# A bidirectional hybrid encoder layer: the start of the kernel in another order, with the conditioning row by transfer, one shift column on TensorE, h in pairs, and x of groups 2 and 3 issued later

## Chip, cores and metric

One core of a Trainium2 chip runs the kernel. The metric is the device time of one execution, in microseconds. A run of a kernel's time is the median of several executions; the profile is of one more execution, and its span goes from the first to the last instruction.

## The reference, cut to what matters

One layer over 2048 tokens of 1024 channels. The part that the change touches is the modulated norm at the layer's start and the first columns of the input projection:

```python
c_act = silu(c)
mod = c_act @ w_ada + b_ada
shift, scale, gate = split(mod, 3)
h = rmsnorm(x, norm_w) * (1.0 + scale) + shift
proj = h @ w_in + b_in                  # 4624 columns
# neighbourhood attention and a chunked two-way mLSTM on parts of proj
y = concatenate([na_out, ml_out]) @ w_out
out = rmsnorm(x + gate * y, final_norm_w)
```

`norm_w` times 1 + scale is called `gT` below, one number for each channel, and shift `shT`. Both are needed before h, and h before any product of the projection.

## The kernel before

The tokens go in four groups of 512 (four tiles of 128 each), the channels in eight pieces of 128, called k. A matrix product in float32 is made of three products of rounded parts: h is held as `hhi` and `hlo`, a weight block as `whi` and `wlo`, and a result is the sum of hi·hi, hi·lo and lo·hi. The input projection goes through weight blocks of 256 columns. Blocks 0, 1 and 2 (values and output gates of the mLSTM heads) are first; block 0 carries the 16 gate columns beside it and is 272 wide.

`start` makes the h of all four groups and applies these first blocks. It is written under a manual schedule: each engine does its instructions in the order of the Python lines. After it, a scheduler orders the instructions by dependence.

The conditioning. The scale and shift of piece k are dot products of silu(c) with 128 columns of `w_ada`. They arrive as 16 pieces of 512 KB (`load_mod(n)`, n = 2k for the scale and 2k + 1 for the shift), in 11 places of which five are used twice. `mod(n)` is one VectorE instruction with a reduction (`dot`, L264) over a piece whose rows are channels and whose 1024 columns meet the silu(c) row, which therefore has to lie in all partitions: `c_all`. In the kernel before, the row comes into one partition (`crow`, L324), gets its Silu, goes to all partitions by two TensorE products with a row of ones (L356), and two ScalarE copies take it out of PSUM (L366). For k = 0 both numbers come from TensorE instead: 8 matmuls of one column each (L381), each in two passes, on matrix pieces laid out the other way. Around these stand filler matmuls (`warm`, L350): 14, then 3, then 2, which write a tile that nothing reads.

Group 0. x is scaled by the norm's factor, turned by TensorE (`turned(k)`, L392, two pieces ahead), and ScalarE makes `hhi` and h from the turned x with gT and shT (`first_h`, L399); VectorE makes `hlo` (L400). `products(k)` (L426) does 24 matmuls for piece k, on blocks 0 (`a`) and 1 (`b`): first those with hhi, then those with hlo. VectorE also does the dots for the next piece and the low parts of the weights (L320).

Groups 1 to 3. x comes a second time, transposed (`load_t`, L254), beside the rows for the norm (`load_x`, L248). `spread` puts the norm's factors in all partitions by four matmuls with a diagonal (L290). `make_h` is three steps for each piece: VectorE multiplies (L406), ScalarE adds the shift and rounds (`hhi`, L407), VectorE takes the difference (`hlo`, L408). They are called from `next_h` for pieces 0 to 3, between the tiles of the block before, and singly for 4 to 7. Tiles for h have two buffers.

Evictions and stores. `vo_group` adds the bias on VectorE (L672) into a staging tile (two exist, used in turn), ScalarE applies a Sigmoid (L678), and the tile is stored to `d_ck`: for group 0 at once, from ScalarE's queue (L681), else later from SP's (L683). An eviction into a staging tile waits until the store before has left it. For group 0 three blocks follow each other (0, 1, 2); for the others two, and block 2 comes again later for groups 1 to 3.

SP issues most transfers, in the order of the program; `table_fills` (L714) are large writes of a constant to DRAM that lie between them. A transfer waits for an earlier one that uses the same of eight semaphores, so up to eight are under way.

## Time and profile before

| | us |
|---|---|
| median of 3 runs | 1343.73 |
| lowest, highest | 1339.22, 1345.5 |
| the profiled execution | 1341.4 |
| its span | 1339.3 |
| TensorE busy in the span | 1290.9 |
| VectorE busy in the span | 796.4 |

How to read the lines below. In the windows view each row is a stretch of the span; the engines stand in the order PE (TensorE's matmuls), PEld (its weight loads), DVE (VectorE), ACT (ScalarE), POOL (GpSimd), each with busy time and number of instructions; then the granted TensorE clock as a share, the mean busy share of the 16 DMA engines and their GB/s. In the timeline each row has start, length, engine, source line, operation, what is written and read, the shape, and how many alike were merged; in brackets the engine's idle time before it and what ended that. SPq and ACTq are issues of transfers. A matmul in float32 appears as two records unless it turns a tile. Mean lengths of matmuls overlap: the distance of their starts is what one costs.

### The profile page before, as it was taken

Reading aid. Unit: us, or ns where it says so; the run is one execution under the profiler, and the core shown is the slowest. Engines: PE = TensorE matmul, PEld = TensorE weight load, DVE = VectorE, ACT = ScalarE, POOL = GpSimd, SP = SyncE. Lnnn points to the kernel's source line nnn. Section 1 sums busy time; section 2 is a strip of 40 time slices with the busy share of each in tenths; the row PEclk is TensorE's granted clock in tenths of the full one; section 3 lists DMA queues with packets and bytes.
Section 4 is the critical chain, followed back from the end, with each engine's and each line's share of the span. In section 5 each row is a group of like instructions: output and inputs, shape, how many; then the busy total and the mean of one; then the engine's idle time right before and its main releaser. Section 6 shows DMA issues by size and latency. Waiting matters only on the chain.

```text
span 1339.3 us, 23091 instructions
## 1 busy us (share of the span) xinstructions
PE 1290.9 (96%) x8174; PEld 1103.9 (82%) x8174; DVE 796.4 (59%) x2447; ACT 537.9 (40%) x1176; POOL 194.3 (15%) x255
## 2 busy tenths in 40 slices
PE   8988899999999999999999999999998999999996
PEld 7888899999888787888878888888876777778785
DVE  4855453222545569166767878777547676766663
ACT  4533331644223233123323323333356555565551
POOL 0000100434000000001212002212202211212211
PEclk8989999999999999999999999999999999999998
DMA  9698883999637685545656867656679877868871
GB/s 363 236 285 248 221 233 101 226 221 236 178 92 222 157 204 163 173 119 150 201 157 202 244 192 220 208 163 181 204 249 229 213 193 194 197 176 193 188 185 47
DMA packets 236822, 263.34 MB, mean 197 GB/s; under 512 B 31127, under 2 KB 192279, under 8 KB 236708
## 3 DMA queue, kind: packets, MB, share of 16 engines
q1 hardware_dynamic: 151758, 188.87, 50.0%
q0 software_dynamic: 20496, 36.21, 11.2%
q10 hardware_dynamic: 64454, 36.80, 9.5%
q8 instruction: 64, 1.05, 0.3%
q14 instruction: 50, 0.41, 0.1%
HBM read 177.28 MB, written 92.72 MB: 202 GB/s over the span
## 4 chain that ended last, share of the span: by engine, by line
PE 66%; DMA 12%; DVE 8%; issue 7%; ACT 5%; POOL 1%; SPq 1%; ACTq 0%; DVEq 0%; POOLq 0%
PE pq L1043 18%; PE y L1622 11%; PE pc L601 4%; PE pc L600 4%; PE pc L602 4%; DMA tab<-d_t 3%; PE pT L1562 3%; PE pO L1577 2%; PE pS L1534 2%; DMA dec<-d_mneg 2%; PE pvo L600 2%; PE pvo L601 2%; PE pvo L602 2%; PE px L1282 2%; PE pi L1284 2%
## 5 line engine op out<-in xcount | busy, mean ns | idle before, releaser
L1043 PE MATMUL pq<-hhi,whi_a 128*128 128x512 f32 x512 | 208.2, 407 | 0.8 <-ACT u L948 0.8
L1043 PE MATMUL pq<-hlo,whi_a 128*128 128x512 f32 x512 | 208.4, 407 | 0.0
L1043 PE MATMUL pq<-hhi,wlo_a 128*128 128x512 f32 x512 | 206.7, 404 | 0.0
L1043 PEld LDWEIGHTS pq<-hhi,whi_a 128*128 128x128 f32 x512 | 96.8, 189 | 17.8 <-ACT u L948 1.3
L1043 PEld LDWEIGHTS pq<-hhi,wlo_a 128*128 128x128 f32 x512 | 96.8, 189 | 16.4
L1043 PEld LDWEIGHTS pq<-hlo,whi_a 128*128 128x128 f32 x512 | 96.7, 189 | 16.0 <-issue 0.5
L1564 ACT ACTIVATE pt<-pT 96x384 f32<-96x384 f32 (+3 forms) x128 | 65.9, 515 | 86.1 <-PE pT L1562 83.6
L1543 ACT ACTIVATE pbuf<-pbuf,mn 128x480 f32<-128x480 f32 (+5 forms) x128 | 76.0, 595 | 52.0 <-DVE mn L1542 52.0
L1622 PE MATMUL y<-hhi,whi_a 128*128 128x512 f32 x256 | 91.7, 420 | 0.5 <-ACT whi_a L1592 0.5
L1622 PE MATMUL y<-hhi,wlo_a 128*128 128x512 f32 (+1 forms) x272 | 90.7, 399 | 0.2 <-ACT y L1629 0.2
L1017 POOL TENSOR_TENSOR wlo_a<-rawq,whi_a 128x1024 fp32r<-128x1024 f32 x19 | 45.5, 2396 | 290.8 <-ACT whi_a L1016 277.4
L1542 DVE CUSTOM_DVE_ANT_0 pbuf<-pS,tab 128x480 f32<-128x480 f32 (+5 forms) x128 | 63.0, 540 | 37.2 <-PE pS L1534 31.3
L1287 ACT ACTIVATE num<-px,gtile 128x129 f32<-128x129 f32 x120 | 38.3, 366 | 113.1 <-PE px L1282 83.5
L1562 PEld LDWEIGHTS pT<-ident,pbuf 128*128 128x128 f32 (+2 forms) x416 | 50.9, 137 | 30.0 <-issue 10.5
L1562 PE MATMUL pT<-ident,pbuf 128*128 128x128 f32 (+2 forms) x416 | 67.2, 275 | 8.5 <-DVE pbuf L1554 7.4
L600 PE MATMUL pvo<-whi_b,hhi 128*128 128x256 f32 x224 | 63.7, 285 | 0.0
L1306 POOL TENSOR_TENSOR hm<-hm,ck 128x128 f32<-128x128 f32 x64 | 26.5, 414 | 254.3 <-DVE hm L1305 223.6
L672 DVE TENSOR_TENSOR stvo<-pvo,brow 128x256 f32<-128x256 f32 x60 | 25.0, 422 | 64.4 <-PE pvo L602 54.6
L602 PE MATMUL pvo<-whi_b,hlo 128*128 128x256 f32 x224 | 63.0, 281 | 0.0
L890 ACT ACTIVATE dec<-dec,gtile 128x128 f32<-128x128 f32 x128 | 42.6, 393 | 50.8 <-POOL dec L883 45.8
L601 PE MATMUL pvo<-wlo_b,hhi 128*128 128x256 f32 x224 | 63.0, 281 | 0.0
L635 DVE TENSOR_TENSOR stv<-pv,brow 128x256 f32<-128x256 f32 x32 | 12.8, 422 | 72.7 <-PE pv L602 47.0
(331 smaller groups left out, 3391.5 us busy)
## 6 DMA issues: line engine op xcount, KB each, us to landing
ck<-d_ck SPq DMA_DIRECT2D x64, 384.5 KB
rawq<-in_w_main_dram SPq DMA_DIRECT2D x28, 512.0 KB
raw<-in_w_main_dram SPq DMA_DIRECT2D x18, 512.0 KB
kv<-d_ck SPq DMA_DIRECT2D x64, 128.5 KB
dec<-d_mneg SPq DMA_DIRECT2D x32, 256.0 KB
d_ck<-dec ACTq DMA_DIRECT2D x32, 256.0 KB
d_qna<-qst ACTq DMA_DIRECT2D x32, 256.0 KB
xr<-in_x_dram POOLq DMA_DIRECT2D x15, 512.0 KB, 8.7
```

The costliest lines, as they stand in the source:

```text
L600: nc.tensor.matmul(ps, lhi(k), rhi(k), start=(k == 0), stop=False)
L601: nc.tensor.matmul(ps, lhi(k), rlo(k), start=False, stop=False)
L602: self.mark = nc.tensor.matmul(ps, llo(k), rhi(k), start=False, stop=(k == KT - 1))
L890: nc.scalar.activation(t[:, o, :], t[:, o, :], AF.Exp, bias=self.cols["g"][:, d, h, c : c + 1])
L1017: (eng or nc.gpsimd).tensor_tensor(lo[:, :, cs], raw, hi[:, :, cs].bitcast(F32), ALU.subtract)
L1043: self.mark = nc.tensor.matmul(patch_ps(ps) if patch else ps, w, self.htok(h, g, k, patch), start=(k == 0 and n == 0), stop=(k == KT - 1 a ...
L1287: nc.scalar.activation(num[:, d, :], px[:, d, :], AF.Copy, scale=self.cols["inter"][:, d, h, c : c + 1])
L1542: nc.vector.tensor_tensor_reduce(pt[:, :nk], ps, tabs[place[u]][j][:, :nk], 1.0, 3e38, ALU.add, ALU.min, mn)
L1543: nc.scalar.activation(pt[:, :nk], pt[:, :nk], AF.Exp, bias=mn, scale=-1.0, accum_out=sums[:, j : j + 1])
L1562: nc.tensor.transpose(ps[:cs, i, :], U[u][j][:, i * cs : (i + 1) * cs], self.ident)
L1564: nc.scalar.activation(t[:cs, :nch, :], ps[:cs, :nch, :], AF.Copy)
L1622: nc.tensor.matmul(y, m[:, k, :], w[k][:, cs], start=(k == 4 and n == 0), stop=(k == 3 and n == 2))
```

## The change

1. The conditioning row is no longer spread by TensorE. SP loads it into all 128 partitions at once (a transfer that reads the one row 128 times), behind the first two matrix pieces, the first weight piece and the gate columns. ScalarE applies the Silu to the 128x1024 tile inside the loop, at k = 0. `crow`, its Silu, the two products and the two copies are gone.
2. Of the 19 filler matmuls 5 are left, all at the start.
3. The small VectorE step for `nwb` stands behind the norm's factors instead of ahead of the squares.
4. The shift of piece 1 comes from TensorE: a third column product (piece n = 3, laid out for it on the host) in the middle of `products(0)`, which does all 12 matmuls of block 0 first, then this column, then the 12 of block 1. ScalarE adds the bias. `mod(3)` is gone from VectorE, and `mod(5)` is done at k = 1.
5. `make_h` returns its last step, and `next_h` runs pieces 0 and 1, and 2 and 3, as pairs.
6. `load_x(2)` and `load_t(2)` stand behind the third block of group 0, `load_x(3)` in group 1; the store of that third block goes to SP's queue.

```diff
-        crow = ada.tile([1, D], F32, name="crow")
-        nc.scalar.dma_start(crow, self.c_row)
...
         nc.sync.dma_start(rg, self.w_gate)
+        nc.sync.dma_start(cb, self.c_row.broadcast_to([P, D]))
         load_p(1, 0)
...
-        nc.scalar.activation(crow, crow, AF.Silu)
-        cbs = []
-        for j in range(2):
-            cbs.append(self.tq.tile([P, GT], F32, tag="tp", name=f"cb_{j}"))
-            nc.tensor.matmul(cbs[j], self.ones[0:1, :], crow[:, j * GT : (j + 1) * GT], start=True, stop=True)
-        warm(14)
+        for _ in range(5):
+            nc.tensor.matmul(dense[:, :240], self.ident, self.big, start=True, stop=True)
...
-        nc.vector.scalar_tensor_tensor(nwb, badd[:, KT:], 1.0, nw, ALU.add, ALU.mult)
         for tt in (0, 2):
             square(tt, ssq)
-            if tt == 0:
-                for j in range(2):
-                    nc.scalar.copy(cb[:, j * GT : (j + 1) * GT], cbs[j])
             dot(xt[tt + 1], xt[tt + 1], 1.0, 0.0, ssq[:, tt + 1 : tt + 2])
         rst = roots(four, ssq)
+        nc.vector.scalar_tensor_tensor(nwb, badd[:, KT:], 1.0, nw, ALU.add, ALU.mult)
...
+        def column(to, n):
+            for kt in range(KT):
+                nc.tensor.matmul(to, places[n][:, kt * P : (kt + 1) * P], cact[:, kt : kt + 1], start=kt == 0, stop=kt == KT - 1)
         for e in range(2):
-            if e:
-                warm(3)
+            column(sums[:, e : e + 1], e)
...
-            nc.vector.scalar_tensor_tensor(lo, h, self.shT[:, k : k + 1], hi.bitcast(F32), ALU.add, ALU.subtract)
+            return lambda: nc.vector.scalar_tensor_tensor(lo, h, self.shT[:, k : k + 1], hi.bitcast(F32), ALU.add, ALU.subtract)
...
+            if k == 0:
+                turns.sort(key=lambda t: t[0])
+            for i, (b, o, n) in enumerate(turns):
+                if k == 0 and i == 12:
+                    column(sums[:, 0:1], 3)
...
             if k == 0:
-                low_p = split_p(1, 0)
+                low()
+                split_p(1, 0)()
+                nc.scalar.activation(cb, cb, AF.Silu)
...
                 mod(2 * k + 2)
-            low()
-            if k == 0:
-                low_p()
-            if k + 1 < KT:
+            if k == 1:
+                mod(5)
+            if k:
+                low()
+            if 1 < k < KT - 1:
                 mod(2 * k + 3)
...
             products(k)
+            if k == 0:
+                nc.scalar.activation(self.shT[:, 1:2], sums[:, 0:1], AF.Identity, bias=badd[:, 1:2])
...
-        load_x(2)
         self.small_loads()
-        load_t(2)
-        load_x(3)
...
             for k in (0, 2):
-                make_h(tiles, k)
-                make_h(tiles, k + 1)
+                for low in (make_h(tiles, k), make_h(tiles, k + 1)):
+                    low()
                 yield
...
                 if g == 1:
+                    load_x(3)
                     load_t(3)
...
                 self.vo_group(2, 2, 0, brow=brow, tops=tops)
                 self.wslot.pop()
+                load_x(2)
+                load_t(2)
...
-            nc.scalar.dma_start(dst, st[:, :, 0:257])
+            (nc.sync if h == 2 else nc.scalar).dma_start(dst, st[:, :, 0:257])
```

Three places show what this does to the order on the engines. The first is TensorE's program from its start to the first products; `mod` is the tile of the columns (16 matmuls are two columns), `tp` the turned x, `pvo` the results of blocks 0 and 1. Before:

```order
1 L356 MATMUL cb_198<-crow,ones 128x512
2 L356 MATMUL cb_200<-crow,ones 128x512
3 L350 MATMUL dense<-big,ident 128x240 x14
4 L381 MATMUL mod_252<-cact,mod_hi 128x1 x8
5 L350 MATMUL dense<-big,ident 128x240 x3
6 L381 MATMUL mod_252<-cact,mod_hi 128x1 x8
7 L350 MATMUL dense<-big,ident 128x240 x2
8 L392 MATMUL tp_0_278<-ident,x_166 128x128
```

And the same place with the change:

```order
1 L347 MATMUL dense<-big,ident 128x240 x5
2 L366 MATMUL mod_235<-cact,mod_hi 128x1 x16
3 L380 MATMUL tp_0_256<-ident,x_164 128x128
4 L380 MATMUL tp_0_256<-ident,x_166 128x128
5 L380 MATMUL tp_0_256<-ident,x_168 128x128
```

The end of the products with block 0, the third column, and the start of block 1, with the change:

```order
20 L418 MATMUL pvo_1_267<-whi_a,hlo_103 128x272
21 L418 MATMUL pvo_2_268<-whi_a,hlo_103 128x272
22 L418 MATMUL pvo_3_269<-whi_a,hlo_103 128x272
23 L366 MATMUL mod_287<-cact,mod_hi 128x1 x8
24 L418 MATMUL pvo_0_201<-whi_b,hhi_102 128x256
25 L418 MATMUL pvo_0_201<-wlo_b,hhi_102 128x256
```

The columns now stand directly behind five fillers, and a third one lies between the products of block 0 and those of block 1, which before were mixed.

The second place is VectorE in the third block of group 0, where the h of group 1 is made; `stvo` rows are evictions. Before:

```order
95 L672 TENSOR_TENSOR stvo_0_701<-pvo_2_757,brow_x 128x2x128
96 L406 SCALAR_TENSOR_TENSOR h_0_783<-xt_624,gT,rb_698 128x512
97 L408 SCALAR_TENSOR_TENSOR hlo_623<-h_0_783,shT,hhi_622 128x512
98 L406 SCALAR_TENSOR_TENSOR h_1_787<-xt_624,gT,rb_698 128x512
99 L408 SCALAR_TENSOR_TENSOR hlo_623<-h_1_787,shT,hhi_622 128x512
100 L672 TENSOR_TENSOR stvo_0_701<-pvo_3_791,brow_x 128x2x128
```

With the change:

```order
93 L671 TENSOR_TENSOR stvo_0_670<-pvo_2_726,brow_x 128x2x128
94 L394 SCALAR_TENSOR_TENSOR h_0_752<-xt_611,gT,rb_667 128x512
95 L394 SCALAR_TENSOR_TENSOR h_1_755<-xt_611,gT,rb_667 128x512
96 L396 SCALAR_TENSOR_TENSOR hlo_610<-h_0_752,shT,hhi_609 128x512
97 L396 SCALAR_TENSOR_TENSOR hlo_610<-h_1_755,shT,hhi_609 128x512
98 L671 TENSOR_TENSOR stvo_0_670<-pvo_3_760,brow_x 128x2x128
```

Both multiplications of a pair now stand ahead of both differences.

The third place is SP's queue behind the transposed x of group 1 (`xt`, four transfers). `x_638` and the next are x of group 2, `x_rows` x of group 3, `d_t` the fills. Before:

```order
33 L254 DMA xt_624<-in_x_t_dram 128x1024 x4
34 L248 DMA x_638<-in_x_dram 128x1024
35 L248 DMA x_640<-in_x_dram 128x1024
36 L248 DMA x_642<-in_x_dram 128x1024
37 L248 DMA x_644<-in_x_dram 128x1024
38 L131 DMA bcol<-in_b_col_dram 128x24
```

With the change, from the table's first small fills (`d_e`, which the scheduler has drawn ahead) on:

```order
41 L694 DMA d_e_73<-big 256x1x240
42 L694 DMA d_e_74<-big 256x1x180
43 L680 DMA d_ck<-stvo_0_670 128x4x257
44 L248 DMA x_796<-in_x_dram 128x1024
45 L248 DMA x_798<-in_x_dram 128x1024
46 L248 DMA x_800<-in_x_dram 128x1024
47 L248 DMA x_802<-in_x_dram 128x1024
48 L254 DMA xt_804<-in_x_t_dram 128x1024 x4
49 L713 DMA d_t_75<-big 2048x1x132
50 L248 DMA x_rows<-in_x_dram 128x1024 x4
```

x of group 2 now stands behind the store of the third block (`d_ck`), and x of group 3 behind the first fill.

More of the change, by code (lines that the diff above doesn't have):

```diff
@@ L346, in start @@
         dense = self.pp.tile([P, GT], F32, tag="pp", name="dense")
-        def warm(n):
-            for _ in range(n):
-                nc.tensor.matmul(dense[:, :240], self.ident, self.big, start=True, stop=True)
-        nc.scalar.activation(crow, crow, AF.Silu)
-        cbs = []
-        for j in range(2):
-            cbs.append(self.tq.tile([P, GT], F32, tag="tp", name=f"cb_{j}"))
-            nc.tensor.matmul(cbs[j], self.ones[0:1, :], crow[:, j * GT : (j + 1) * GT], start=True, stop=True)
-        warm(14)
+        for _ in range(5):
+            nc.tensor.matmul(dense[:, :240], self.ident, self.big, start=True, stop=True)
         banks = [self.tq.tile([P, GT], F32, tag="tb", name=f"pvo_1_{i}") for i in range(2)]
@@ L506, in start @@
                     if k < 3:
-                        make_h(now, k + 5)
+                        make_h(now, k + 5)()
                     if k == 2:
@@ L535, in start @@
             if tiles:
-                make_h(tiles, 4)
+                make_h(tiles, 4)()
             if g == 1:
```

10 lines of the change are left out of this document (5 added, 5 removed).

## The prediction

> **What bounds the kernel now.** The page first: one engine carries the span.
>
> ```profile
> span 1339.3 us, 23091 instructions
> PE 1290.9 (96%) x8174; PEld 1103.9 (82%) x8174; DVE 796.4 (59%) x2447; ACT 537.9 (40%) x1176; POOL 194.3 (15%) x255
> ```
>
> TensorE is busy for 96%, so time can be won where it idles or does filler work. Next the stages, in the windows view (end of the preparation, of group 0, of its third block, of groups 1, 2, 3; columns: stretch, busy time of each engine, granted clock, DMA share, GB/s).
>
> ```profile
> 0.00:26.50 26.50, 21.34 (x83) 16.91 (x83) 8.53 (x27) 8.48 (x16) 1.03 (x9) 0.91 0.94 352
> 26.50:59.50 33.00, 30.48 (x216) 28.96 (x217) 30.52 (x53) 21.81 (x33) 0.00 (x0) 0.92 0.62 232
> 59.50:72.10 12.60, 12.58 (x106) 12.38 (x104) 3.52 (x19) 3.17 (x5) 0.10 (x1) 1.00 0.95 361
> 72.10:92.55 20.45, 15.42 (x98) 14.76 (x99) 13.58 (x25) 8.59 (x14) 0.21 (x2) 0.83 0.93 285
> 92.55:122.10 29.55, 26.02 (x203) 24.70 (x202) 17.36 (x45) 11.40 (x19) 0.21 (x2) 1.00 1.00 268
> 122.10:151.50 29.40, 25.91 (x202) 24.59 (x201) 17.23 (x44) 8.97 (x14) 1.06 (x5) 1.00 0.70 195
> 151.50:200.00 48.50, 47.38 (x392) 46.17 (x392) 22.69 (x70) 19.86 (x24) 5.10 (x6) 1.00 0.86 249
> ```
>
> Before 26.5 TensorE does no product of the block matmuls. From 26.5 to 59.5 VectorE is the fullest engine (30.5 of 33.0 us); from 72 to 151 nothing is full, which is the mark of a chain of waits. After 151 TensorE is full again, so what is won before 151 should arrive at the end. All terms lie before 151.
>
> **Preparation: first product from 26.5 to about 19.3.** Timeline rows:
>
> ```profile
> 8.79 8.87 PE L350 MATMUL dense<-big,ident 128*128 128x240 f32 x28
> 12.44 0.63 ACT L319 ACTIVATE whi_a<-raw 128x512 fp32r<-128x512 f32 x1 [1.91 <-DMA raw<-in_w_main_dram]
> 17.50 1.84 PE L381 MATMUL mod<-cact,mod_hi 128*128 128x1 f32 x16
> 24.50 1.91 PE L392 MATMUL tp<-ident,x 128*128 128x128 f32 x8
> 25.66 0.78 ACT L399 ACTIVATE hhi<-tp,shT,gT 128x512 fp32r<-128x512 f32 x1 [2.22 <-PE tp L392]
> 26.49 0.60 PE L426 MATMUL pvo<-whi_a,hhi 128*128 128x272 f32 x1
> ```
>
> The first column product (the scale of piece 0) starts at 17.5, behind the filler; its data is there much earlier: the weight piece that SP issues behind the two matrix pieces lands at 12.4, a 256 KB transfer takes about 0.65 us at the 404 GB/s that row 21.60:28.40 below shows, so piece two is there at about 11.75 and piece one (512 KB, 1.3 us) at 10.4. The filler that is left (5 of 19) ends near 6. Between lies idle time, so I price the two columns at half clock, from these rows (the view of one line: ns min/median/max, first and last start; then two windows with the granted clock):
>
> ```profile
> L381 PE MATMUL mod<-cact,mod_hi x16: 167/250/250, 17.5 to 19.1; 128*128 128x1 f32 x16
> L381 PE MATMUL mod<-cact,mod_hi x6: 303/352/352, 21.5 to 22.6; 128*128 128x1 f32 x6
> L426 PE MATMUL pvo<-wlo_a,hhi x4: 374/432/432, 26.9 to 28.2; 128*128 128x272 f32 x4
> 14.80:21.50 6.70, 6.70 (x46) 6.45 (x45) 3.54 (x8) 0.24 (x2) 0.00 (x0) 1.00 1.03 412
> 21.60:28.40 6.80, 6.72 (x27) 5.96 (x27) 1.25 (x3) 3.24 (x7) 0.00 (x0) 0.50 1.03 404
> ```
>
> At full clock the 16 half-products of a column start over 1.6 us (17.5 to 19.1: 0.107 apart); at half clock 5 intervals take 1.1 us (0.21 apart), 3.4 us a column. So the columns run 10.4 to 17.3, then four turns of x (0.85 at half clock, half of the 1.91 row), and the gap from the first turn to the first product stays as it is (24.50 to 26.49, 2.0): 19.3. Nothing that makes the other inputs moves back by more than the one short step for nwb, and in the old run they stood ready while ScalarE's first h waited for the turns (2.22). **Gain 7.2 us at this point.**
>
> Most of it does not last. The shift of piece 1 moves from VectorE to a third column, in the middle of the products of piece 0, and everything there is still at half clock: 12 products of 272 columns at 0.22 (in the row 26.9 to 28.2 every second one starts 0.44 after the last), 2.7 us, to 22.0; the column, 3.4, to 25.45; 12 products of block 1 at 0.21, 2.6, and the turns for piece 2, to 28.75. The products of piece 1 begin there; now at 30.77. **Two us are left on TensorE.**
>
> ```profile
> 40.00:50.00 10.00, 9.59 (x76) 9.02 (x75) 9.77 (x17) 5.21 (x8) 0.00 (x0) 1.00 0.01 2
> 30.77 0.37 PE L426 MATMUL pvo<-whi_a,hhi 128*128 128x272 f32 x1
> 34.13 0.37 PE L426 MATMUL pvo<-whi_a,hhi 128*128 128x272 f32 x1
> 34.24 1.34 DVE L264 CUSTOM_DVE_ANT_0 junkv<-mod_lo,c_all,nwb 128x1024 bf16<-128x1024 f32 x1
> 52.82 0.09 DVE L264 DVE_READ_ACCUMULATOR2_ANT shT<- 128x1 f32 x1
> 53.83 0.39 PE L426 MATMUL pvo<-whi_a,hhi 128*128 128x272 f32 x1 [0.83 <-ACT hhi L399]
> ```
>
> VectorE's own chain: its first dot now waits for the conditioning row's Silu on ScalarE (about 21.6, behind h of piece 0 and a weight split), then dots for pieces 2, 4, 5 at 1.3 each to 25.7, the low part of piece 1 when its shift is there (the column at 25.45, two activations of 0.77, so 27.3 to 28.0), two splits to 29.2. There begins the dot that begins at 34.24 now: **5.0 us earlier**, and its unchanged work (34.24 to 52.82) ends at 47.8. TensorE needs 3.36 for a piece (30.77 to 34.13), so from 28.75 six pieces (the sixth without turns) end at 48.5. The two meet; piece 7 starts at about 49.1 for 53.83, and with the same tail the third block starts at **54.9 for 59.5: 4.6 us won.**
>
> What costs nothing here: the broadcast of the row (512 KB, 1.3 us at 404 GB/s; above, at a quarter of that rate, 5.2) delays every later transfer by as much. By 40 the queue is empty (share 0.01 in the row 40.00:50.00), and the matrix pieces wanted at 21.6 and 22 would land at about 16 and 17 (12.4, then 64 KB, the row, 256 KB and 512 KB each), or 20 and 21 at the slow end. Silu of 128x1024 takes what a Square does (1.05, below) while TensorE is on the third column. Gone beside that: two copies, one Silu, 14 fillers, one dot (1.28).
>
> **The write-out wait: 3.5 us.** Rows of the timeline and one of the chain of waits (the third column is what held the chain), and two later stores with the instruction that waits for each:
>
> ```profile
> 55.29 1.05 ACT L260 ACTIVATE junk<-x 128x1024 bf16<-128x1024 f32 x1
> 62.15 9.69 DMA d_ck<-stvo
> 71.97 1.09 DVE L672 TENSOR_TENSOR stvo<-pvo,brow_x 128x256 f32<-128x256 f32 x3 [8.45 <-DMA d_ck<-stvo]
> 72.97 0.74 DVE L406 SCALAR_TENSOR_TENSOR h<-xt,gT,rb 128x512 f32<-128x512 f32 x1
> 124.86 0.36 SPq L683 DMA_DIRECT2D d_ck<-stvo  x1
> 128.24 0.11 POOL L661 MEMSET stvo<- 128x4 f32 x1 [11.85 <-DMA d_ck<-stvo]
> 140.89 0.37 SPq L683 DMA_DIRECT2D d_ck<-stvo  x1
> 147.64 0.10 POOL L661 MEMSET stvo<- 128x4 f32 x1 [19.30 <-DMA d_ck<-stvo]
> ```
>
> The third block writes into the staging tile that block 0's store must empty first; that store takes 9.7 us beside 2 MB of x of group 2, VectorE waits for it, and the h of group 1 stands behind the waiting eviction. The change issues that x after the third block. Alone, such a store took 3.4 us (124.86 to 128.24), beside fills 6.7. The x of group 1, its squares and the Sigmoid ahead of the store hang on the loop and move 4.5 us with it: issued at 57.7 it lands between 61.1 and 64.4. Three of four tiles of the third block (12.6 us, row 59.50:72.10) are done at 54.9+9.5 = 64.4. I take no wait; the upper end costs 0.8. h then starts at 64.8 where it starts at 72.97: 8.2, of which 4.6 is counted, **3.5 to 3.6 new.**
>
> The Trainium skill, "DMA: Bandwidth & Descriptors", section "Queues, rings and completion order", has each DMA engine alternate between the ScalarE and SP rings packet by packet. By it the store would not wait for the whole x, and removing x would win perhaps half. The 9.69 row disagrees; the sum by the page would be 1.8 less.
>
> **Pairs of h: 9 us.** Grouped rows from 72.9 to 149.9, and one step:
>
> ```profile
> L408 DVE SCALAR_TENSOR_TENSOR hlo<-h,shT,hhi 128x512 fp32r<-128x512 f32 x24 | 18.0, 752 | 19.0 <-ACT hhi L407 19.0
> 102.38 0.74 DVE L406 SCALAR_TENSOR_TENSOR h<-xt,gT,rb 128x512 f32<-128x512 f32 x1
> 103.91 0.75 DVE L408 SCALAR_TENSOR_TENSOR hlo<-h,shT,hhi 128x512 fp32r<-128x512 f32 x1 [0.79 <-ACT hhi L407]
> 104.58 0.74 DVE L406 SCALAR_TENSOR_TENSOR h<-xt,gT,rb 128x512 f32<-128x512 f32 x1
> ```
>
> VectorE idles 19.0 us for the ScalarE step, 0.79 in each of 24. In a pair the second h (0.67) fills the first wait and the first low part the second: 2.89 for two in place of 4.40, 1.51 saved. Two pairs in each of groups 1, 2, 3 (pieces 4 to 7 stay single): **9.1 us.** Is the chain the bound? The group period is 29.5 now and 26.5 then; TensorE is busy for 26.0 of it, so the chain stays the bound, if barely.
>
> **Later transfers.** x of groups 2 and 3 (8.4 MB) now goes behind the third block's store, which SP issues after ScalarE's Sigmoid at about 71 (64.8, two pairs, an eviction). Behind the store's 3.4 us eight transfers at 1.3 to 1.5 land from 76 to 86; squares of group 2 begin at 79 (h of group 1 takes 15.0: two pairs, an eviction of 0.4, four times 2.2) and take 1.2 each, and its h begins at 91. Both are covered, by 2 to 5 us. In all 20.8 MB (x, five stores, seven fills) go out up to the weights of block 2; at 315 GB/s, between the rows with 268 and 361, they end at 137, about when those weights are issued. These now take 7.3 us:
>
> ```profile
> 152.49 0.90 SPq L208 DMA_DIRECT2D raw<-in_w_main_dram  x2
> 159.84 1.06 ACT L212 ACTIVATE whi_a<-raw 128x1024 fp32r<-128x1024 f32 x1 [4.73 <-DMA raw<-in_w_main_dram]
> ```
>
> Cost taken 0; from -1 (two transfers fewer ahead of them) to 8 (at 268 GB/s the 20.8 MB end at 149, less the 4 us or so that TensorE can wait).
>
> **Sum.** 4.6 + 3.5 + 9.1 = 17.2 us. The profiled execution took 1341.4 us (span 1339.3), which gives 1324.2; from the median of 1343.7 it would be 1326.5. I give 1325.
>
> **Rivals.**
> - *The clock returns early* (0.08): if half of the 6.8 us that the slow stretch lasted is enough, full clock is back at about 22.7, the third column is 2.0 instead of 3.4 and the products behind it half as long; 2 us earlier, 1323. Against it: in 21.60:28.40 TensorE is busy for 6.72 of 6.80 us and stays at 0.50. The Trainium skill, "TensorE: Matmul & The Clock Gate", section "What's actually happening", has the full clock back after about 3.4 us of sustained work; by that rule, this is the time, and the row disagrees.
> - *The pairs bring nothing* (0.07): if TensorE or ScalarE sets the group period, 9.1 goes; 1333. For it: TensorE idles only 3.5 in 29.5. Against: VectorE's 0.79 before each of 24 low parts, all put down to ScalarE.
> - *Transfers become the bound* (0.15): 268 GB/s holds, the weights of block 2 land up to 8 late; 1332. For it: share 1.00 from 92 to 122 with the work now pressed into less time; against: share 0.70 after.
> - *The gain is given back later* (0.07): a later stage that waits for transfers and not for TensorE swallows over 10; 1336 to 1341. Against: the last row of the windows.
> - *Slower* (0.03): the same queue. x of group 2 starts at 71 instead of during the old run's third block, and the h of groups 2 and 3 hang on it. To lose 17.2 and 6.7 more, the 20.8 MB have to end 24 us late: 90 us for them, under 231 GB/s at full share; then 1348 or more. No row at share near 1 is under 268.
>
> Forecast: 0.60. Faster by over 0.5% (6.7 us, about what a measurement of this kernel can tell from no change) is forecast, clock, most of transfers and of pairs: 0.87; within 0.5%: 0.10; slower: 0.03. Range 1316 (clock early, all stores hidden, a fast run) to 1334 (pairs or transfers).
>
> **What would show it.** First product near 19.3; third column at half clock; the third block's first product near 55; no VectorE wait of 8 us for the store; two h rows in a row and 26.4 us between the ends of groups; weights of block 2 within 5 us of their issue; TensorE's idle time after 151 unchanged. A first store landing after 66, or squares of group 2 waiting for x, would make it wrong.

## The result, and the profile after

| | kernel before | changed kernel | ratio, 95% interval |
|---|---|---|---|
| first comparison (10 runs each) | 1344.41 us | 1333.87 us (1327.63 to 1339.23) | 0.9917, 0.9890 to 0.9943 |
| repeat 1 (17 and 4 runs) | 1342.06 | 1328.11 | 0.9891, 0.9834 to 0.9948 |
| repeat 2 (18 and 6 runs) | 1341.32 | 1327.03 | 0.9903, 0.9866 to 0.9940 |

The change makes the kernel faster by 10.5 to 14.3 us, 0.8 to 1.1%. The forecast was 1325, 17.2 us won. The profiled execution took 1328.0 us.

The head of the page of the changed kernel, and its windows view, cut at the same events as the windows of the kernel before (same columns):

```profile
span 1326.2 us, 23060 instructions
...
PE 1282.2 (97%) x8158; PEld 1099.5 (83%) x8158; DVE 791.9 (60%) x2445; ACT 536.6 (40%) x1175; POOL 194.9 (15%) x255
```

```profile
0.00:18.40 18.40, 13.14 (x50) 11.56 (x50) 7.30 (x25) 6.21 (x13) 1.02 (x9) 1.00 0.91 335
18.40:52.10 33.70, 31.89 (x233) 30.98 (x234) 30.77 (x53) 23.08 (x35) 0.00 (x0) 0.95 0.88 334
52.10:64.65 12.55, 12.55 (x107) 12.55 (x107) 6.79 (x24) 4.40 (x7) 0.21 (x2) 1.00 0.76 256
64.65:78.68 14.03, 13.11 (x99) 12.23 (x98) 10.19 (x19) 7.09 (x12) 0.10 (x1) 1.00 0.68 237
78.68:105.20 26.52, 25.42 (x201) 24.32 (x199) 16.55 (x43) 11.31 (x19) 0.10 (x1) 1.00 1.09 309
105.20:132.60 27.40, 25.65 (x202) 24.81 (x203) 17.56 (x47) 8.82 (x14) 0.21 (x2) 1.00 1.12 321
132.60:182.00 49.40, 47.60 (x393) 46.20 (x393) 22.49 (x70) 19.85 (x24) 6.10 (x10) 1.00 0.92 246
```

The preparation is 8.1 us shorter (18.4 for 26.5), group 1 is 6.4 shorter (14.03 for 20.45) and groups 2 and 3 are 3.0 and 2.0 shorter (26.52 for 29.55, 27.40 for 29.40). The loop of group 0, which now holds the third column, is 0.7 longer (33.70 for 33.00); 2.6 were forecast. In the third block's row VectorE's work has doubled (6.79 for 3.52): the first pair of h of group 1 now lies inside it. By 200 us the changed kernel is 18 us ahead. The clock of 1.00 in the first row is no measurement: in this profile the records of the granted clock begin at 21.43 us, and ahead of them the view shows 1.00.

The steps themselves: TensorE's timeline at the start, then VectorE's timeline at the two waits for a store, then VectorE's low parts of h (view of groups, 62.1 to 131.1).

```profile
9.59 6.96 PE L366 MATMUL mod<-cact,mod_hi 128*128 128x1 f32 x32 [3.65 <-DMA mod_hi<-in_w_mod_dram]
...
18.43 0.60 PE L418 MATMUL pvo<-whi_a,hhi 128*128 128x272 f32 x1
...
21.31 1.90 PE L366 MATMUL mod<-cact,mod_hi 128*128 128x1 f32 x16
...
24.93 0.37 PE L418 MATMUL pvo<-whi_a,hhi 128*128 128x272 f32 x1
...
52.08 0.32 PE L599 MATMUL pvo<-w_extra,hhi 128*128 128x256 f32 x1
```

```profile
59.12 0.76 DVE L671 TENSOR_TENSOR stvo<-pvo,brow_x 128x256 f32<-128x256 f32 x2 [3.01 <-DMA d_ck<-stvo]
61.83 0.43 DVE L671 TENSOR_TENSOR stvo<-pvo,brow_x 128x256 f32<-128x256 f32 x1 [1.95 <-PE pvo L601]
62.17 1.40 DVE L394 SCALAR_TENSOR_TENSOR h<-xt,gT,rb 128x512 f32<-128x512 f32 x2
...
115.04 1.09 DVE L671 TENSOR_TENSOR stvo<-pvo,brow 128x256 f32<-128x256 f32 x3 [4.61 <-DMA d_ck<-stvo]
116.04 1.40 DVE L394 SCALAR_TENSOR_TENSOR h<-xt,gT,rb 128x512 f32<-128x512 f32 x2
```

```profile
L396 DVE SCALAR_TENSOR_TENSOR hlo<-h,shT,hhi 128x512 fp32r<-128x512 f32 x24 | 17.5, 751 | 10.3 <-ACT hhi L395 9.5
```

Two columns together take 6.96, 3.48 each: by their length half clock, as forecast. The first product stands at 18.43 (forecast 19.3). The third column takes 1.90: full clock, where half was forecast. The store that held the third block for 8.45 us still holds it for 3.01, but TensorE's third tile ends later than the store does (VectorE waits 1.95 for it after the first two evictions), so h waits for TensorE. The low parts wait 10.3 us for ScalarE instead of 19.0. New is the wait at 115.04: a later store holds h of group 3 for about 1.1 us.

Then the gain shrinks. Three later places show it, in the timelines of VectorE, TensorE and ScalarE (one fence for each engine):

```profile
312.67 1.42 DVE L634 TENSOR_TENSOR stv<-pv,brow 128x256 f32<-128x256 f32 x4 [12.01 <-DMA d_vna<-stv]
```

```profile
313.14 0.39 PE L599 MATMUL pv<-whi_b,hhi 128*128 128x256 f32 x1 [2.69 <-DVE stv L634]
...
446.72 0.66 PE L995 MATMUL kt<-ident,acc_k 128*128 128x128 f32 x4 [2.46 <-ACT acc_k L986]
...
965.59 0.53 PE L1561 MATMUL pT<-ident,pbuf 128*96 128x128 f32 x3 [2.54 <-ACT pt L1563]
```

```profile
445.46 0.60 ACT L997 ACTIVATE stk<-kt 128x512 f32<-128x512 f32 x1 [3.89 <-DMA d_ck<-stk]
...
965.05 0.49 ACT L1563 ACTIVATE pt<-pT 96x384 f32<-96x384 f32 x1 [3.77 <-issue]
```

At 313 VectorE waits 12 us for the store of v; it then clears four tiles at once (x4), since TensorE has filled all its banks and stood still for 2.69. At 446 ScalarE waits for a store of k and TensorE behind it; at 965 ScalarE is busy issuing transfers. In the kernel before TensorE waits at the same instructions for nothing (0.59 two groups of tiles earlier), 1.15 and 1.09 us.

The next table is worked out from the traces: for the 8,100 TensorE instructions that all these programs have (all but the fillers, the columns and the row's spreading), the end in one trace less the end in the first profile of the kernel before. Shown is how much each stretch (cut at that profile's times, us) is shorter (-) or longer (+) than in that profile.

| one profile each | to 60 | 60-165 | 165-290 | 290-480 | 480-950 | 950-1180 | to the end | all |
|---|---|---|---|---|---|---|---|---|
| before, second profile | -4.2 | +1.1 | 0 | +1.3 | -0.1 | -0.9 | -1.1 | -3.7 |
| before without table rows | -0.1 | +0.2 | 0 | -2.8 | -0.6 | -0.2 | -1.6 | -5.0 |
| before + pairs | -1.6 | -8.1 | -0.9 | +1.7 | -0.5 | -0.9 | -1.0 | -11.1 |
| **changed** | -7.4 | -10.8 | +0.1 | +4.8 | -0.7 | +1.8 | -1.0 | -13.1 |
| changed, second | -6.3 | -10.8 | 0 | +2.1 | +1.1 | +9.3 | -0.3 | -4.9 |
| changed, third | -7.3 | -11.9 | +0.1 | +0.6 | -0.5 | 0 | +1.7 | -17.3 |
| changed, h single | -7.6 | -3.3 | 0 | +5.9 | +1.6 | +7.0 | -1.4 | +2.3 |
| changed, x early | -9.3 | -6.9 | 0 | +2.5 | -0.3 | +3.9 | -0.6 | -10.7 |
| changed, v by ScalarE | -7.8 | -11.2 | +0.3 | +5.1 | -0.4 | +4.3 | -0.4 | -10.0 |
| changed, 9 fillers | -9.5 | -12.0 | +0.1 | +3.8 | +0.9 | +1.2 | -0.5 | -15.9 |
| changed, all pairs | -7.8 | -11.8 | 0 | +6.9 | -0.2 | +9.4 | -1.2 | -4.7 |
| changed without table rows | -6.8 | -12.0 | 0 | -2.8 | -1.5 | +4.0 | -0.8 | -20.0 |

Up to 290 us the three profiles of the changed kernel agree within 2 us: 17.1 to 19.1 won. Behind that they win nothing more and lose 2 to 12. Each row is one execution, and not always one near the median: the one of h single took 1343.66, and its median is 1333.37.

### The profile page after: what moved, and what is told of

The parts are those of the page before. It is cut to its first block, busy times and chain, and to the rows that moved or that the text cites. A ratio compares the mean times of both kernels' runs of the same rounds, so it can differ in the third digit from the quotient of the medians.

```text
span 1326.2 us, 23060 instructions
## 1 busy us (share of the span) xinstructions
PE 1282.2 (97%) x8158; PEld 1099.5 (83%) x8158; DVE 791.9 (60%) x2445; ACT 536.6 (40%) x1175; POOL 194.9 (15%) x255
## 3 DMA queue, kind: packets, MB, share of 16 engines
q0 software_dynamic: 20496, 36.21, 11.1%
## 4 chain that ended last, share of the span: by engine, by line
PE 62%; DMA 21%; issue 7%; DVE 5%; ACT 2%; POOL 1%; SPq 1%; ACTq 0%; POOLq 0%; DVEq 0%
PE pq L1042 19%; PE y L1621 10%; DMA tab<-d_t 5%; PE pc L600 4%; PE pc L599 4%; PE pc L601 4%; DMA d_ck<-dec 3%; PE pT L1561 2%; PE pO L1576 2%; DMA dec<-d_mneg 2%; PE pi L1283 2%; PE px L1281 2%; PE pS L1533 2%; PE pvo L599 2%; PE pvo L600 2%
## 5 line engine op out<-in xcount | busy, mean ns | idle before, releaser
L671 DVE TENSOR_TENSOR stvo<-pvo,brow 128x256 f32<-128x256 f32 x60 | 24.9, 421 | 64.1 <-PE pvo L601 47.0
```

## The experiments

Times are medians. Each is compared with the kernel before as it ran beside it on the same chip: 1342.06 for the first four experiments, 1342.47 for the next four, 1341.32 for the last four. In brackets stand the ratio to it and its 95% interval.

**The changed kernel again** (no edit).

> The changed kernel once more, unaltered. Theory A (the opening brings what the sum says or a little more, about 18 to 19 us by the end of group 3's h; a part is given back later at fixed places): the lead of TensorE over the kernel before is again 17 to 19 us from 165 to 300 us, and TensorE again waits 2 to 3.5 us near 310 us for VectorE, which waits for the store of v; the time is 1327 to 1338. Theory B (nothing is given back at a fixed place; the loss after 150 us is the luck of one execution): no wait over 1 us near 310, and the losses lie at other places.

1328.11 us. The wait near 310 is there again (2.24 us before the product at 313.65), so theory A holds there; but the same profile loses 9.3 us between 950 and 1180, where the first one lost 1.8. VectorE's timeline there and TensorE's at the start:

```profile
1151.84 0.56 DVE L1541 CUSTOM_DVE_ANT_0 pbuf<-pS,tab 128x384 f32<-128x384 f32 x1 [1.88 <-DMA tab<-d_t]
```

```profile
21.57 3.41 PE L366 MATMUL mod<-cact,mod_hi 128*128 128x1 f32 x16
...
1154.17 0.87 PE L1561 MATMUL pT<-ident,pbuf 128*128 128x128 f32 x3 [3.45 <-DVE pbuf L1553]
```

A table that lands late (tab) holds VectorE in steps, and TensorE for 3.45. The third column takes 3.41 here and 1.90 in the first profile: the same program at another clock.

**h single again.**

```diff
-                for low in (make_h(tiles, k), make_h(tiles, k + 1)):
-                    low()
+                make_h(tiles, k)()
+                make_h(tiles, k + 1)()
```

> The changed kernel with every h made singly again. By the sum of the prediction the pairs are worth 1.5 us each, 9.1 us by the end of group 3's h: that end near 140 instead of 131, group periods near 29.4, and the time 7 to 9 us above the changed kernel run beside it. If the gain is given back later anyway (transfers of the table stage set the pace there), the end of group 3 moves by 9 but the time only by 4 to 6. If the pairs bring nothing, both stay.

1333.37 us (0.9938, 0.9907 to 0.9969). The last low part of group 3 (VectorE's timeline):

```profile
138.18 0.75 DVE L396 SCALAR_TENSOR_TENSOR hlo<-h,shT,hhi 128x512 fp32r<-128x512 f32 x1 [0.79 <-ACT hhi L395]
```

It ends at 138.9 for 131.0, 7.9 later: the 9.1 of the sum less the 1.1 that the changed kernel loses at 115 and this one, with its slower chain, does not. At the end the medians differ by 5.3 us (1328.11 for the changed kernel beside it). That is what the second branch of the expectation says, but the two intervals overlap: by the times alone neither 9 nor nothing is excluded.

**x of groups 2 and 3 early again.**

```diff
+        load_x(2)
         self.small_loads()
+        load_t(2)
+        load_x(3)
...
                 self.wslot.pop()
-                load_x(2)
-                load_t(2)
...
                 if g == 1:
-                    load_x(3)
                     load_t(3)
```

> The changed kernel with the loads of x for groups 2 and 3 issued where they stood before (ahead of the small loads); the store of the third block stays on SP. By the sum, the first store lands 8 to 10 us after its issue again, VectorE waits about 8 us for it, h of group 1 begins 3.4 us later (65.6 instead of 62.2) and the time is 3 to 4 us above the changed kernel. If the store was not what held h (or the transfers are covered elsewhere), h of group 1 stays at 62 and the time stays. If the later wait for the store of group 1 (1.1 us at 115) goes with it, 1.1 of the 3.4 comes back.

Chain of waits (start, us, what), then VectorE's timeline:

```profile
54.57 9.52 DMA d_ck<-stvo
```

```profile
64.22 1.09 DVE L671 TENSOR_TENSOR stvo<-pvo,brow_x 128x256 f32<-128x256 f32 x3 [8.51 <-DMA d_ck<-stvo]
65.22 1.40 DVE L394 SCALAR_TENSOR_TENSOR h<-xt,gT,rb 128x512 f32<-128x512 f32 x2
```

The store takes 9.52 us again (9.69 in the kernel before, 4.4 in the changed one), VectorE waits 8.51, and h begins 3.05 later. The place and the size were right: between 60 and 165 us this profile wins 3.9 us less than the first one of the changed kernel. Yet the time is 1327.61 (0.9881, 0.9847 to 0.9915), as good as the changed kernel's: at the end nothing of this loss can be seen.

**The stores of v on ScalarE's queue.**

```diff
-        self.defer(lambda: nc.sync.dma_start(dst, st[:, :, :256]))
+        self.defer(lambda: nc.scalar.dma_start(dst, st[:, :, :256]))
```

> The changed kernel with the stores of v (blocks 4 and 5) issued on ScalarE's queue instead of SP's, where each stands behind table loads that wait for earlier transfers. Theory A with SP's order as the cause: the wait near 310 us goes, TensorE's lead stays 18 us up to 440 us, and the time is 2 to 3 us below the changed kernel. Theory A with the rate of the transfers as the cause: the store leaves earlier but lands as late, and 1 us or less is won. Theory B: no difference.

VectorE's timeline:

```profile
323.09 1.42 DVE L634 TENSOR_TENSOR stv<-pv,brow 128x256 f32<-128x256 f32 x4 [11.59 <-DMA d_vna<-stv]
```

The wait does not go, it comes one group of tiles later (TensorE loses 2.37 there, 5.1 in the stretch from 290 to 480). But the edit did not make the store leave early. ScalarE's timeline ahead of it:

```profile
312.68 1.80 ACT L889 ACTIVATE dec<-dec,gtile 128x128 f32<-128x128 f32 x5 [5.06 <-POOL dec L882]
...
316.12 0.52 ACTq L639 DMA_DIRECT2D d_vna<-stv  x1
```

The store stands behind work of ScalarE that waits 5.06 us for GpSimd, and leaves at 316.12, 17 us after the last eviction into its tile; in the changed kernel SP issues the store that VectorE waits for 15.5 us after (303.65 for 288.1). So this run does not decide whether the order of the issues or the transfers themselves are the cause. 1326.91 us (0.9869, 0.9814 to 0.9923), not to be told from the changed kernel.

**The kernel before again** (no edit).

> The kernel before once more, unaltered, for a second profile of it. In the five profiles of kernels with the new opening TensorE waits 1.0 to 3.9 us near 300 to 325 us for the store of v, 1.6 to 2.5 near 446, 1.6 to 2.5 near 965, and in four of them 2.6 to 3.5 near 1152; in the one profile of the kernel before these are 0.6, 1.2, 1.1 and none. If these waits belong to executions and not to the change, the second profile of before shows them too (1.5 us or more at three of the four places, 12 to 15 us later in time; idle time of TensorE after 150 us 20 to 28 us instead of 18.4). If the change causes them, this profile stays near 18.4 and below 1.3 at each of the four.

1341.18 us. TensorE's waits are 1.78 at 304.6, 1.75 near 460, 1.16 near 976 and 1.37 near 1159: over 1.5 at two of the four places, where the expectation asked for three, so single waits do belong to executions. But TensorE's idle time after 150 us is 17.5, no more than in the first profile (18.1); in the three profiles of the changed kernel it is 20.9, 24.9 and 18.3, so two of the three wait longer in sum. New is the opening: 4.2 us shorter in the same program.

**The pairs alone, in the kernel before.**

```diff
+            return lambda: nc.vector.scalar_tensor_tensor(lo, h, ...)
-            nc.vector.scalar_tensor_tensor(lo, h, ...)
...
-                make_h(tiles, k)
-                make_h(tiles, k + 1)
+                for low in (make_h(tiles, k), make_h(tiles, k + 1)):
+                    low()
```

> The kernel before with the pairs alone. By the sum, the last low part of group 3 ends 9.1 us earlier (at 140.8 for 149.9), and TensorE's lead near 200 us is 8 to 9.5 us; what is left at the end is 5 to 9 (1334 to 1339). If the gain of the pairs hangs on the rest of the change (earlier x loads, the store), the end of group 3 moves by less than 6. If TensorE sets the period, by less than 3.

VectorE's timeline:

```profile
140.16 0.75 DVE L408 SCALAR_TENSOR_TENSOR hlo<-h,shT,hhi 128x512 fp32r<-128x512 f32 x1 [0.79 <-ACT hhi L407]
```

The last low part ends at 140.9, as the sum says (140.8). 1329.95 us (0.9901, 0.9873 to 0.9929): 12.5 less than before (9.5 to 17 by the interval), more than its 9, and as much as the whole change. By the medians, pairs and the rest of the change do not add up at the end: 12.5 by the pairs alone, 8.7 by the rest alone, 10.5 to 14.3 together.

**Nine fillers instead of five.**

```diff
-        for _ in range(5):
+        for _ in range(9):
             nc.tensor.matmul(dense[:, :240], self.ident, self.big, start=True, stop=True)
```

> The changed kernel with 9 filler products instead of 5 ahead of the first two columns, so that TensorE is busy from 1.6 to about 9.5 us. In the profiles so far the granted clock changes only on a grid of 3.413 us; a window in which TensorE idles about half or more is followed by one at half clock, a window filled with products by one at full. By that, full clock is there when the columns begin at about 9.6: at full clock all the way they take 3.7 us instead of 6.96, and as columns do not count as work the clock falls again inside them or behind them: 4 to 5.5 us, the first product at 15 to 17 instead of 18.4, the third block's first product 0 to 2.5 us earlier, the time 0 to 2.5 us below the changed kernel. If the clock only depends on products of the matrix pieces, nothing changes.

TensorE's timeline:

```profile
9.84 4.66 PE L366 MATMUL mod<-cact,mod_hi 128*128 128x1 f32 x32 [2.42 <-DMA mod_hi<-in_w_mod_dram]
...
16.38 0.59 PE L418 MATMUL pvo<-whi_a,hhi 128*128 128x272 f32 x1
```

The columns take 4.66 for 6.96, the first product stands 2.05 earlier, and 2.1 us are kept through the opening. 1325.42 us (lowest 1325.15, highest 1328.06; 0.9875, 0.9851 to 0.9899): the interval lies below 1 but overlaps those of the changed kernel, so the 2.1 us are shown by the trace and not by the time.

**Without the rows of the position tables.** The 72 transfers of d_t from d_e are left out.

```diff
-        for r in range(8):
+        for r in range(0):
             row = 8 * pr + r
```

> The changed kernel without the 72 transfers that copy the rows of the position tables (d_t from d_e), so the tables keep their fill value and what is computed from them differs. These transfers run beside the stores of v between 235 and 335 us, at a DMA share near 1. If the rate of the transfers in that stage is what takes back the lead near 310 us, the wait for the store of v falls below 0.6 us, the store lands within 5 us of its issue and TensorE's lead over the kernel before stays at 18 us up to 440. If it is SP's order or chance, the wait stays at 1 us or more.

1320.33 us (0.9827, 0.9795 to 0.9858). VectorE's timeline near 310:

```profile
305.37 0.76 DVE L634 TENSOR_TENSOR stv<-pv,brow 128x256 f32<-128x256 f32 x2 [5.46 <-DMA d_vna<-stv]
306.91 0.43 DVE L634 TENSOR_TENSOR stv<-pv,brow 128x256 f32<-128x256 f32 x1 [0.78 <-PE pv L601]
309.76 0.42 DVE L634 TENSOR_TENSOR stv<-pv,brow 128x256 f32<-128x256 f32 x1 [2.42 <-PE pv L601]
```

VectorE is soon back to waiting for TensorE, TensorE waits for nothing between 290 and 480, and that stretch takes 2.8 us less than in the kernel before instead of 0.6 to 4.8 more. So the rows are what makes TensorE wait for the stores of v and k. One part of the expectation missed: the store does not land within 5 us. SP's queue in the changed kernel and in this one, the store that VectorE then waits for:

```profile
303.65 0.37 SPq L639 DMA_DIRECT2D d_vna<-stv  x1
```

```profile
295.70 0.37 SPq L639 DMA_DIRECT2D d_vna<-stv  x1
```

It takes 8.9 us to land with the rows and 9.6 without them, but it leaves SP 8 us earlier without them. The rows cost the store its place in time in the queue and not its own landing; which of SP's waits they lengthen was not separated.

**The same omission in the kernel before.**

> The kernel before without the 72 transfers of the table rows (d_t from d_e); the tables keep their fill value. The changed kernel without them took 1320 us. If these transfers are what takes back the gain of the change (TensorE's lead waits at the stores of v and k, which they delay), the kernel before loses little by them and gains at most 2 to 4 us here: 1337 to 1340, so that the change alone is worth its full 17 to 19 us where the rows are gone. If they cost both kernels the same, 1329 to 1333, and the difference stays 10 to 13 us.

1336.57 us (0.9966, 0.9947 to 0.9986), 4.7 less; the stretch 290 to 480 takes 2.8 less than in the first profile, as it does in the changed kernel without rows. Without the rows the change is worth 0.9827/0.9966 = 0.986, 18.6 us, the size of the sum; with them 0.989 to 0.992. The stretch is shown directly; by the medians alone the two sizes lie within each other's intervals (an estimate from the two intervals: 0.986 has about 0.004 to either side).

**The changed kernel a third time** (no edit).

> The changed kernel once more, unaltered, beside the next two on the same chip: 1327 to 1335, 9 to 14 us below the kernel before. In its profile: waits of 1.5 us or more for the store of v near 311, for a store of k near 446, and at 965; each window of the 3.413 us grid in which TensorE idles over 1.7 us is followed by one at half clock, any with under 1.6 by one at full clock.

1327.03 us. TensorE waits 0.89 for the store of v at 310.26, not over 1.5; 1.54 for that of k and 1.81 at 959. The expectation of a fixed wait near 311 missed here; that executions fall on both sides where the slack is about zero is an argument, not a measurement. The rule for the clock held in this profile but for one case of the mixed zone below (1.81 idle, then full).

**All eight pieces of h in pairs.**

```diff
-                    if k < 3:
-                        make_h(now, k + 5)()
+                    if k == 0:
+                        lows = [make_h(now, n) for n in (6, 7)]
+                        for low in lows:
+                            low()
...
-                make_h(tiles, 4)()
+                lows = [make_h(tiles, k) for k in (4, 5)]
+                for low in lows:
+                    low()
```

> The changed kernel with pieces 4 to 7 of h in pairs too (4 with 5, 6 with 7), in groups 1 to 3. VectorE's chain loses another 1.5 us per pair, up to 9 us in three groups; but TensorE is busy for 26.0 of the group period, which is 26.4 now. By the prediction's account (TensorE nearly the bound) the period falls to 25.9 to 26.2 and the whole gains 0 to 1.5 us. If TensorE is not the bound, the period falls to 23.5 and the time by 5 to 8.

Windows from h of group 1 to that of group 2, and on to group 3; then VectorE's timeline:

```profile
61.80:86.60 24.80, 24.71 (x203) 24.50 (x202) 16.80 (x44) 11.20 (x18) 0.10 (x1) 1.00 0.76 228
86.60:115.25 28.65, 26.19 (x213) 25.78 (x213) 16.75 (x46) 11.19 (x18) 0.21 (x2) 1.00 1.10 318
```

```profile
114.25 1.09 DVE L675 TENSOR_TENSOR stvo<-pvo,brow 128x256 f32<-128x256 f32 x3 [6.32 <-DMA d_ck<-stvo]
```

In the first period TensorE is busy for 24.71 of 24.80: it is the bound, 1.5 us below the 26.35 of the changed kernel. The second gives 1.1 of that back (28.65 for 27.52): VectorE waits for the store of group 1, which lands 11.2 us after its issue, at DMA share 1.10. 1331.52 us (0.9914, 0.9882 to 0.9946): nothing won.

**Table rows one block later, with nine fillers.**

```diff
-        for _ in range(5):
+        for _ in range(9):
...
-            nc.sync.dma_start(
+            step = nc.sync.dma_start(
...
+            self.behind(step, self.mark)
...
-            for rt in range(3):
-                if i < 3:
-                    self.tables_rows(i, rt)
...
                     self.ch_tile(ps, self.wslot[slot], sub, g)
+                    if i and 4 * sub + g in (0, 2, 4):
+                        self.tables_rows(i - 1, (4 * sub + g) // 2)
```

`behind` keeps the scheduler from drawing a row ahead of the products that stand before it.

> The changed kernel with 9 fillers, and with the table rows issued one block later each (in blocks 7, 8 and 9 of the matrix, spread over them, in place of at the head of blocks 6, 7 and 8), away from the stores of v. With 9 fillers alone the time was 1325.4. If the rows beside the stores of v are what stops TensorE near 310, that wait falls below 0.6 us and 2 to 4 us are won: 1321 to 1324. If the rows then delay the stores of k or q instead, the wait turns up between 380 and 520 and nothing is won.

1353.79 us, slower than before (1.0091, 1.0059 to 1.0122). TensorE waits for nothing from 290 to 440, the stretch with the stores of v, but later (SP's queue, then TensorE's timeline):

```profile
475.25 6.91 SPq L726 DMA_DIRECT2D d_t<-d_e  x8
...
529.37 13.69 SPq L726 DMA_DIRECT2D d_t<-d_e  x8
```

```profile
512.49 0.80 PE L1042 MATMUL pq<-hhi,whi_a 128*128 128x512 f32 x1 [6.68 <-ACT u L947]
...
557.18 0.79 PE L1042 MATMUL pq<-hhi,whi_a 128*128 128x512 f32 x1 [19.74 <-ACT whi_a L1015]
```

Eight rows in a run hold SP for 7 to 14 us, and a matrix piece of the next stage stands behind them: it leaves at 549.84 and TensorE waits 19.74 us for it. At the first place TensorE waits 6.68 for ScalarE; that chain was not followed to its start. So the move to this place, eight rows at a time, costs more than it saves.

## Why the prediction was right in kind and its gain 3 to 7 us too high

- **What bounds the kernel: right.** The gain was won up to 165 us, where TensorE idled.
- **Preparation and loop, 4.6: mis-sized.** Measured 6.3 to 7.4 against the first profile of before, and 5.5 between the means of the three profiles of the changed kernel (-7.0) and of the four with the old opening (0, -4.2, -0.1, -1.6). Two steps of the sum failed, both on the clock. The first is "everything there is still at half clock": the third column took 1.90 and 1.84 us in two profiles and 3.41 in one. The first product of piece 7 in the first profile and in the repeat (TensorE's timelines; the sum has it at 49.1):

```profile
46.41 0.39 PE L418 MATMUL pvo<-whi_a,hhi 128*128 128x272 f32 x1 [0.84 <-ACT hhi L387]
```

```profile
49.03 0.39 PE L418 MATMUL pvo<-whi_a,hhi 128*128 128x272 f32 x1
```

At half clock the sum is right to 0.1 us; full clock is worth 2.6. That was the first rival: its price, 2 us, was about right, its chance of 0.08 too low. I had ruled it out with the row 21.60:28.40, in which TensorE is busy for 6.72 of 6.80 at clock 0.50. But its first 1.2 us are column products, which are busy in the profile and seem not to count for the clock (below). The second step is "with the same tail": the 5.7 us from piece 7 to the third block of the kernel before hold a window at half clock (55.73 to 59.14). The first and the third profile have such a window too (from 48.7 and 48.6) and the same tail; the repeat has none, and its tail is 4.2. So the two cases lie only 1.1 apart at 60 us, and both win more than 4.6.
- **Write-out wait, 3.5: right.** 3.4 in the profile (h 10.8 earlier, the third block 7.4), 3.05 by the experiment. "I take no wait" held for h: VectorE waited 3.01 for the store, but TensorE's third tile came later still.
- **Pairs, 9.1: right.** 9.0 in the kernel before with the pairs alone; low parts wait 10.3 instead of 19.0. "Barely" was right too: TensorE is busy for 24.71 of 24.80 as soon as the chain is shorter.
- **Later transfers up to block 2, 0: nearly right.** The weights were issued at 134.52 and ScalarE's first part began at 141.65, 7 us as before. Missed was the store that lands at 114.9 and costs group 3 1.1 us. The reading "no row at share near 1 is under 268" holds for the long rows shown; from 90 to 100 us the same trace has 250 GB/s at share 0.98.
- **"What is won before 151 should arrive at the end": this step failed.** 17 to 19 us were there at 290; 10.5 to 14.3 arrive. The fourth rival had the mechanism, with a chance of 0.07, and at over 10 us where 3 to 7 went; it lost against one row (151 to 200) that I let speak for all the rest. The later cost was in no term of the sum. The place was in the old trace, in VectorE's timeline of the kernel before:

```profile
328.50 1.42 DVE L635 TENSOR_TENSOR stv<-pv,brow 128x256 f32<-128x256 f32 x4 [8.88 <-DMA d_vna<-stv]
```

VectorE waits 8.88 us for the store of v there, clears four tiles at once, and TensorE goes on without a gap: the fourth bank was just being filled. A wait of that length that costs nothing is a wait without slack. The two runs without the rows show that the rows use it up (290 to 480: TensorE does not idle in either).
- **The range.** The median of the first comparison, 1333.87, lies 0.13 us inside the range's upper end of 1334. That end was priced for pairs that bring nothing or for transfers as the bound up to block 2. Neither happened; that the loss at later places came to about as much is luck.
- **Open:** from 950 to 1180 the nine profiles with the new opening in the table lose 0 to 9.4 us (eight of them over 1), the four with the old one nothing (-0.9 to 0). At 965 ScalarE's five issues take until 965.05 from 960.24, 4.8 us for 3.4 in the kernel before; five of the other profiles with the new opening have 3.6 to 4.0, but the first of the five issues takes 1.22 in each of them and 0.73 or 0.74 with the old opening. Near 1151 the tables that VectorE waits for land 10.8 to 12.7 us after their issue in the repeat, h single, x early and all pairs, and 9.2 to 10.1 in the three profiles with the old opening that wait for one. Why was not found, and no run varies it.

## What to carry to other kernels

A gain in front of a long pipeline has to pass the later places that have no slack: look in the old trace for engines that wait long for a store while TensorE does not, and put the loss there into the sum. Parts that each win alone need not add up: run each alone, and run the kernel without what is suspected to use up the gain. Compare several profiles of the same program before putting a price on a stretch whose clock changes.

## What the runs showed of the hardware

In all fourteen profiles the granted clock changes only on a grid of 3.413 us, whose position differs from run to run, and how long TensorE idles in one window of the grid goes with the clock of the next. Two windows views cut on the grid, of the changed kernel and of its repeat (columns as above; the second figure is TensorE's busy time):

```profile
444.68:448.09 3.41, 1.37 (x8) 1.24 (x9) 2.58 (x4) 1.79 (x3) 0.00 (x0) 1.00 1.18 147
448.09:451.50 3.41, 3.41 (x9) 2.66 (x9) 1.91 (x5) 1.78 (x3) 0.00 (x0) 0.50 0.94 286
```

```profile
442.99:446.41 3.42, 1.77 (x8) 1.12 (x6) 3.42 (x8) 1.13 (x3) 0.00 (x0) 1.00 1.19 193
446.41:449.82 3.41, 3.28 (x16) 2.76 (x17) 1.95 (x4) 2.33 (x5) 0.00 (x0) 1.00 1.04 238
```

The wait at 446 left 2.04 us of a window idle in one run and 1.64 in the other; only the first was followed by a window at half clock. An estimate of what such a window costs is half of it, another 1.7 us. Over all fourteen profiles, between 20 and 1300 us and with the clock full: 30 windows with 1.89 us or more idle were all followed by half clock, 101 with 0.9 to 1.58 never, 37 between them went both ways.

Coming back asks for more: behind 30 us, all 41 half-clock windows with 0.50 us or less idle were followed by full clock, all 15 with 0.59 or more by another at half (so the 6.8 us at half in the repeat at 1153, where the first of the two had TensorE busy for 2.20). A gap that falls across two windows can cost only itself: the 2.69 us at 313 left 1.59 of one window idle, and full clock followed. Much of the spread of one program goes with the clock: in the ten runs of the result the two with a mean clock of 0.993 took 1328.0 and 1327.6 us, the two with 0.984 1339.2 and 1336.1. That the clock makes all of this difference is not shown, since long waits lower it and cost time by themselves.

Products of one column seem not to count as work: in the four profiles with the old opening the window that holds most of the first two columns (18.18 to 21.59 in the first) is full of products. Where TensorE did nothing but columns for 1.95, 1.95 and 1.82 us of it, half clock followed; where it did for 1.67, full clock did, as with idle time of that length. That gives 2.6 of the 4.2 us between the two profiles of the kernel before (first product at 23.85 for 26.49); the rest is the window at 55.73, which the second lacks. One window of the opening does not fit: from 16.33 to 19.74 of the repeat TensorE did other work than columns for all but 0.41 us, and half clock stayed.

The Trainium skill, "TensorE: Matmul & The Clock Gate", section "What's actually happening", describes the free-running window of 3413 ns; the traces agree. It has the clock fall after an idle window and return after a busy one; here just over half an idle window was enough for the fall, and the return needed one that was nearly full.
